# Head of a decoder trunk: half of c spread by a broadcast load, other buffers for the first adaLN tiles, operand parts made straight from x

## The chip, the core and the metric

The kernel runs on one core of one Trainium2 chip. The metric is device time in microseconds (us). A core has five engines that run side by side, each with its own list of instructions: TensorE (PE, matmuls; its weight loads are shown apart as PEld), VectorE (DVE), ScalarE (ACT), GpSimd (POOL) and SyncE (SP). Loads and stores are issued from the lists of SP, ACT and POOL and are carried out by 16 DMA engines. On-chip memory has 128 partitions; matmuls add up in PSUM banks.

## The reference

One layer on 512 tokens of width 2048: a token mixer (stick-breaking attention, sparse attention with a token indexer, gates) and a gated convolutional MLP, each behind an RMS norm whose scale and shift come from a condition vector c (adaLN). What matters here is the start:

```python
c_act = jax.nn.silu(c)
mod = c_act @ w_ada[layer] + b_ada[layer]
sh1, sc1, gt1, sh2, sc2, gt2 = jnp.split(mod[:, None, :], N_MOD, axis=-1)
h = rmsnorm(x, g_mix[layer]) * (1 + sc1) + sh1
...
proj = h @ w_in            # the indexer's queries qi are among its columns
```

## The kernel before, in words

Python code lists the work, tile by tile; a planner of the framework then puts the instructions on the engines' lists. It plays the program through with costs of its own and takes, of what is ready, what stands first in the code, so an engine's list need not have the order of the code. A buffer is asked for by a tag, and each tag has a fixed number of buffers: `raw` 8 (128 x 1024 numbers, 512 KB, for weights as loaded), `wh` and `wl` 3 each (a weight block's high and low part), `F` 62 (128 x 512), `ta`, `w`, `T` 2 each. An instruction that writes into a buffer waits until the last user of that buffer is done.

Matmuls are done in fp32 by parts. A number is written as a high part (rounded by ACT to the matmul type) and a low part (the rest, subtracted on DVE), and `mm3` does three matmuls: high by high, high by low, low by high. `parts` (L133, L135) makes both for a weight block, `split` (L162, L164) for an operand.

The head has these steps.

1. `c_spread` brings SiLU(c), 2048 numbers, into all 128 partitions, as two tiles `cb` of 1024 columns in `raw` buffers. c is loaded as two rows of one partition (L316). A matmul with a column of ones copies each 512 columns to all partitions (L322), ACT does the SiLU out of PSUM (L323). In the profile each of these four matmuls has two records. `cb` is kept, since later stages use it too.
2. An adaLN tile `t` gives 128 entries of `mod`: `ada_half` loads half of the tile's weights (128 x 1024, 512 KB) and multiplies it on DVE by `cb[half]` with a sum along the row (L290); `ada_end` adds the two sums and the bias (L304).
3. Loop over k = 0..15, the 128-row blocks of the model width. Tile 16 + k gives the scale of block k; `amp` (L385) is g_mix times one plus that scale. x of block k (256 KB) is loaded by `next_x`, one block ahead, and squared by ACT (L363), and the squares are added on DVE (L365). The operand of block k is x times amp in high and low part. Then a block of w_qi (128 x 896, 448 KB) is loaded and put into parts, and 21 matmuls of 512 columns add into seven PSUM banks. The norm's factor is applied later.
4. The next stage (`w_va`, 16 blocks) does the same with the normed x and eight banks, and makes the tiles of the shift beside it.

All loads named here are issued from the list of SP.

Of the kernel before, what the change touches and what calls it, by code (L numbers as in the profile page):

```python
# [10 lines left out]
F32 = mybir.dt.float32  # L11
F32R = mybir.dt.float32r
BF16 = mybir.dt.bfloat16
I32 = mybir.dt.int32
AF = mybir.ActivationFunctionType
ALU = mybir.AluOpType
PSUM = bass.MemoryType.PSUM

P = 128
D = 2048  # L20
S = 512
# [55 lines left out]
def block_kernel(ctx: ExitStack, tc: tile.TileContext, A: dict, out: bass.AP):  # L77
    nc = tc.nc
# [6 lines left out]
    def nm(s):  # L85
        counter[0] += 1
        return f"{s}_{counter[0]}"

    def t2k(tag, bufs, dt=F32, w=S):
        return sb.tile([P, w], dt, tag=tag, bufs=bufs, name=nm(tag))  # L90

    def slot(dt=F32):

        return t2k("F", SLOTS, dt)

    def acc():
        return pp.tile([P, S], F32, tag="acc", bufs=3, name=nm("acc"))
# [7 lines left out]
    mm = nc.tensor.matmul  # L105
    act = nc.scalar.activation
    tt = nc.vector.tensor_tensor
    ts = nc.vector.tensor_scalar
    stt = nc.vector.scalar_tensor_tensor
# [28 lines left out]
    def prep(src, w=1024):  # L138
        return parts(load(src, w), w)

    def mm3(ps, lhs, rhs, first, last, check=True):
        (ah, al), (bh, bl) = lhs, rhs
        mm(ps, ah, bh, start=first, stop=False, skip_group_check=not check)  # L143
        mm(ps, ah, bl, start=False, stop=False, skip_group_check=not check)  # L144
        return mm(ps, al, bh, start=False, stop=last, skip_group_check=not check)  # L145

    def cols(w, k, n=P):
        return tuple(x[:, k * n : (k + 1) * n] for x in w)
# [11 lines left out]
    def split(src, hi=None, lo=None):  # L160
        hi = slot(F32R) if hi is None else hi
        pins["hi"] = act(hi, src, AF.Copy)  # L162
        lo = slot(F32R) if lo is None else lo
        tt(lo, src, hi.bitcast(F32), ALU.subtract)  # L164
        return hi, lo
# [119 lines left out]
    amp = sb.tile([P, 2, KT], F32, tag="amp", name="amp")  # L285

    def ada_half(cb, t, half, tag=("raw", 8)):
        raw = t2k(*tag, w=1024)
        nc.sync.dma_start(raw, A["w_ada"][t * P : (t + 1) * P, half * 1024 : (half + 1) * 1024])
        return stt(raw, raw, 1.0, cb[half], ALU.mult, ALU.mult, accum_out=macc[:, t, half : half + 1])  # L290

    @contextmanager
    def behind(*pins):

        with ExitStack() as stack:
            for p in pins:
                stack.enter_context(tc.issue_after(p.ins))
            yield

    def ada_end(a, b):  # L300

        o = mod[:, a:b]
        if b - a == 1:
            stt(o, macc[:, a, 0:1], macc[:, a, 1:2], b_ada[:, a:b], ALU.add, ALU.add)  # L304
        else:
            tt(o, macc[:, a:b, 0], macc[:, a:b, 1], ALU.add)
            tt(o, o, b_ada[:, a:b], ALU.add)

    def c_spread():

        one = t2k("T", 2)[:1, :P]
        nc.vector.memset(one, 1.0)
        cb = []
        rows = [t2k("raw", 8, w=1024) for _ in range(2)]
        for half, row in enumerate(rows):
            nc.sync.dma_start(row[:1], A["c"][:, half * 1024 : (half + 1) * 1024])  # L316
        for row in rows:
            c = t2k("raw", 8, w=1024)
            for i in range(2):
                at = slice(i * S, (i + 1) * S)  # L320
                ps = acc()
                mm(ps, one, row[:1, at], start=True, stop=True)  # L322
                act(c[:, at], ps, AF.Silu)  # L323
            cb.append(c)
        return cb

    cb = c_spread()
    c_col = sb.tile([P, KT], F32, tag="c_col", name="c_col")
    nc.scalar.dma_start(c_col, A["c_col"])
# [3 lines left out]
    def rms(squares, blocks=range(NQB), bank=outs):  # L333

        total = bank()
        at = slice(blocks[0] * P, (blocks[-1] + 1) * P)
        for b in blocks:
            for i, t in enumerate(squares):
                mm(total[:, b : b + 1], t[:, b * P : (b + 1) * P], ones[:, :1], start=b == blocks[0] and i == 0,
                   stop=i == len(squares) - 1, skip_group_check=True)  # L340
        r = sb.tile([P, NQB], F32, tag="r", bufs=2, name=nm("r"))
        rb = r[:, blocks[0] : blocks[-1] + 1]
        act(rb, total[:, blocks[0] : blocks[-1] + 1], AF.Sqrt, scale=1.0 / D, bias=eps)
        nc.vector.reciprocal(rb, rb)
        wide = t2k("T", 2)
        for b in blocks:
            ts(wide[:, b * P : (b + 1) * P], ident, r[:, b : b + 1], None, ALU.mult)
        yield
        out = bank()
        mm(out[:, at], ones, wide[:, at], start=True, stop=True)  # L350
        yield out


    xt, total = [], None
# [3 lines left out]
    def next_x():  # L358
        x = slot()
        nc.sync.dma_start(x, A["x"][len(xt)])  # L360
        xt.append(x)
        sq = t2k("w", 2) if total else t2k("T", 2)
        act(sq, x, AF.Square)  # L363
        if total:
            tt(total, total, sq, ALU.add)  # L365
        return total or sq

    total = next_x()
    for k in range(KT):
        x = xt[k]  # L370
        if k == 6:
            past = t2k("w", 2)[:, :P]
            with behind(pins["load"]):
                nc.sync.dma_start(const, A["consts"][:, :5])
                nc.sync.dma_start(past, A["consts"][:, 5])
            nc.gpsimd.tensor_copy(mask[:, 0, :], ident)
            nc.gpsimd.tensor_copy(mask[:, 1, :], past)
        t = KT + k
        for half in range(2):
            ada_half(cb, t, half)  # L380
        if k == KT - 1:
            norm = rms([total])
            next(norm)
        ada_end(t, t + 1)
        stt(amp[:, 0, k : k + 1], mod[:, t : t + 1], 1.0, g_mix[:, k : k + 1], ALU.add, ALU.mult)  # L385
        h0 = t2k("ta", 2)
        act(h0, x, AF.Copy, scale=amp[:, 0, k : k + 1])
        h0 = split(h0)
        w = prep(A["w_qi"][k], NQ * P)
        for j in range(NQ):  # L390
            mm3(qi_ps[j], cols(w, j), h0, k == 0, k == KT - 1)
            if k == KT - 1 and j == 0:
                rstd = t2k("T", 2)
                act(rstd, next(norm), AF.Copy)
        for _ in range(2 if k == 8 else 1):
            if len(xt) < KT:
                total = next_x()
# [7 lines left out]
    def modulate(x, k, which, h, at=slice(0, S)):  # L405
        xn = t2k("w", 2)
        tt(xn[:, at], x[:, at], rstd[:, at], ALU.mult)
        act(h[:, at], xn[:, at], AF.Identity, scale=amp[:, which, k : k + 1],
            bias=mod[:, 48 * which + k : 48 * which + k + 1])
        return h  # L410
# [22 lines left out]
    for k in range(KT):  # L433
# [6 lines left out]
        w = prep(A["w_va"][k])  # L440
# [17 lines left out]
    ps = acc()  # L458
    for c in range(2):
        w = prep(A["w_tail"][c], 8 * TN)  # L460
# [7 lines left out]
    for j, (src, dst) in enumerate(((A["w_qi7"], qid[7]), (A["w_x0"][0], xd[0]), (A["w_x0"][1], xd[1]))):  # L468
        ps = (acc, att)[j % 2]()
        for c in range(2):  # L470
            w = prep(src[c])
            for k in range(8):
                i = 8 * c + k
# [494 lines left out]
    for j in range(KT):  # L968
        t = t2k("w", 2)
# [3 lines left out]
        ps = acc()  # L973
        w = prep(A["w_b"][j])
# [162 lines left out]
    for j in range(KT):  # L1137
# [5 lines left out]
        x = slot()  # L1143
# [15 lines left out]
    for p in range(KT // 2):  # L1159
        for k in (2 * p, 2 * p + 1):  # L1160
            if k < AHEAD:
                plain(k, [(L, modulated(k, L))], first_w[k])
            elif k % 2:
                x = split(modulate(x1[k], k, 1, x1[k]))
# [42 lines left out]
    for j in range(NU, NJ):  # L1207
        if j < 2 * NU:
            finish(j - NU, *ups[2 * (j - NU) : 2 * (j - NU) + 2])
        elif j < 2 * NU + 2:  # L1210
            x = t2k("T", 2)
# [10 lines left out]
    def bank(b):  # L1222
        return [att() for _ in range(4)] if b % 2 == 0 else [acc() for _ in range(3)] + [outs()]
# [202 lines left out]
    def rows_of(src):  # L1426

        both = [t2k("raw", 8, w=1024) for _ in range(2)]
        for v, r in enumerate(both):
            nc.sync.dma_start(r, src[:, v * 1024 : (v + 1) * 1024].to_broadcast([P, 1024]))  # L1430
        return [both[b // 2][:, b % 2 * S : (b % 2 + 1) * S] for b in range(4)]

    row, g_row = rows_of(gate_row), rows_of(A["g_row"])
# [19 lines left out]
    ps, before = [], None  # L1453
    x1_part = operands(0)
    for t in range(NQB):
# [3 lines left out]
        for b in range(4):  # L1459
            if not ps:  # L1460
                ps = bank(t)
# [3 lines left out]
            x = base[t, b]  # L1465
# [122 lines left out]
```

## Time and profile before

| what | value |
|---|---|
| median of 3 runs | 2807.38 us |
| lowest and highest run | 2806.15 and 2810.97 us |
| span of the profiled execution | 2805.4 us |
| mean granted TensorE clock | 0.997 |
| busy PE / DVE / ACT / POOL | 98% / 86% / 52% / 11% |
| DMA | 549.56 MB, mean 196 GB/s |

The span runs from the first to the last instruction of one execution; the profile gives no other time for that execution, and the median of the runs lies 2.0 us above it. A row of a timeline has the start, the duration, the engine, the line of code, the operation, `output<-inputs`, shapes and a count; in square brackets stand the idle time of the engine before it and what ended it. A row of groups has the busy time and the mean duration in ns at its end. In a row of DMA issues the last number is the time from issue to landing in us. `SPq` is the list of SP.

### The profile page before, as it was taken

What the parts mean: (1) busy time and instruction counts of PE and PEld (TensorE: products, weight loads), DVE (VectorE), ACT (ScalarE), POOL (GpSimd) and SP (SyncE); (2) the same over time, 40 slices, a digit from 0 to 9 for tenths busy, and PEclk for the clock granted to TensorE, in tenths of its full rate; (3) what the DMA queues carried; (4) which work ended last, traced back from release to release, by engine and by line L of the source; (5) the groups of instructions that cost most, each with busy time, mean ns of one, the idle gap of its engine ahead of it and who ended that gap; (6) DMA issues with size and microseconds to landing.
All of it is one profiled execution on the core that took longest, in us unless ns stands there. A gap on an engine that the chain in (4) does not pass through costs nothing.

```text
span 2805.4 us, 47711 instructions
## 1 busy us (share of the span) xinstructions
PE 2760.3 (98%) x18708; PEld 2533.1 (90%) x18708; DVE 2416.1 (86%) x3452; ACT 1464.4 (52%) x2062; POOL 314.4 (11%) x519
## 2 busy tenths in 40 slices
PE   9999999999999999999999999999999999999997
PEld 6779999999998768889999999999999998887875
DVE  8978978888887899788888998989898897888876
ACT  5544354455556655434466555555555455546452
POOL 0110000000002111112220000000000000002112
PEclk9999999999999999999999999999999999999998
DMA  9964456655556449766763666565666336468786
GB/s 358 363 231 135 150 173 211 203 180 166 184 198 220 145 168 314 246 215 191 235 222 116 184 168 175 166 175 167 173 166 173 118 121 213 156 181 240 200 241 195
DMA packets 164045, 549.56 MB, mean 196 GB/s; under 512 B 21398, under 2 KB 21782, under 8 KB 163820
## 3 DMA queue, kind: packets, MB, share of 16 engines
q1 hardware_dynamic: 116076, 404.82, 44.0%
q0 software_dynamic: 47152, 141.30, 17.9%
q8 instruction: 147, 2.41, 0.3%
q14 instruction: 78, 0.64, 0.1%
q10 hardware_dynamic: 592, 0.39, 0.0%
HBM read 453.19 MB, written 89.83 MB: 194 GB/s over the span
## 4 chain that ended last, share of the span: by engine, by line
PE 81%; DVE 10%; DMA 4%; issue 3%; ACT 1%; POOL 0%; DVEq 0%; ACTq 0%; POOLq 0%; SPq 0%
PE att L145 13%; PE att L143 12%; PE att L144 12%; PE acc L145 12%; PE acc L144 12%; PE acc L143 12%; DVE wl L135 2%; DVE raw L290 2%; DMA raw<-in_w_down 1%; DVE F L164 1%; PE acc L722 1%; PE acc L816 1%; PE outs L922 1%; DMA F<-sumd 1%; PE outs L144 1%
## 5 line engine op out<-in xcount | busy, mean ns | idle before, releaser
L133 ACT ACTIVATE wh<-raw 128x1024 fp32r<-128x1024 f32 (+2 forms) x792 | 832.4, 1052 | 1029.1 <-PE acc L144 192.8
L135 DVE TENSOR_TENSOR wl<-raw,wh 128x1024 fp32r<-128x1024 f32 (+2 forms) x792 | 956.2, 1210 | 142.2 <-ACT wh L133 133.6
L143 PE MATMUL acc<-F,wh 128*128 128x256 f32 (+1 forms) x2464 | 718.7, 294 | 6.4 <-ACT F L162 5.0
L145 PE MATMUL acc<-F,wl 128*128 128x256 f32 (+1 forms) x2464 | 721.7, 293 | 2.8 <-DVE wl L135 2.8
L144 PE MATMUL acc<-F,wh 128*128 128x256 f32 (+1 forms) x2464 | 721.9, 293 | 0.0
L145 PE MATMUL att<-F,wl 128*128 128x256 f32 (+1 forms) x2448 | 715.9, 292 | 2.4 <-DVE wl L135 2.4
L144 PE MATMUL att<-F,wh 128*128 128x256 f32 (+1 forms) x2448 | 715.8, 292 | 1.2 <-DVE F L164 1.2
L143 PE MATMUL att<-F,wh 128*128 128x256 f32 (+1 forms) x2448 | 711.8, 293 | 1.5 <-DVE sp L273 0.9
L143 PEld LDWEIGHTS acc<-F,wh 128*128 128x128 f32 x2464 | 471.4, 191 | 21.2 <-ACT F L162 6.8
L145 PEld LDWEIGHTS acc<-F,wl 128*128 128x128 f32 x2464 | 471.4, 191 | 13.3 <-DVE wl L135 3.8
L144 PEld LDWEIGHTS acc<-F,wh 128*128 128x128 f32 x2464 | 471.7, 191 | 11.5 <-DVE F L164 1.4
L143 PEld LDWEIGHTS att<-F,wh 128*128 128x128 f32 x2448 | 469.1, 192 | 12.9 <-issue 3.2
L144 PEld LDWEIGHTS att<-F,wh 128*128 128x128 f32 x2448 | 469.2, 192 | 12.2 <-DVE F L164 4.3
L145 PEld LDWEIGHTS att<-F,wl 128*128 128x128 f32 x2448 | 468.9, 192 | 11.4 <-DVE wl L135 3.4
L290 DVE SCALAR_TENSOR_TENSOR raw<-raw,raw 128x1024 f32<-128x1024 f32 x156 | 187.8, 1217 | 9.1 <-ACT raw L323 7.9
L143 PE MATMUL att<-wh,F 128*128 128x512 f32 x448 | 178.2, 398 | 1.1 <-ACT wh L133 1.1
L144 PE MATMUL att<-wl,F 128*128 128x512 f32 x448 | 175.0, 391 | 0.8 <-DVE wl L135 0.8
L145 PE MATMUL att<-wh,F 128*128 128x512 f32 x448 | 174.8, 390 | 0.0
L233 DVE TENSOR_TENSOR raw<-raw,raw 128x1024 f32<-128x1024 f32 x80 | 97.4, 1217 | 32.4 <-DMA raw<-in_w_o 17.5
L144 PE MATMUL acc<-wl,F 128*128 128x512 f32 x288 | 113.0, 392 | 2.5 <-DVE wl L135 2.5
L143 PE MATMUL acc<-wh,F 128*128 128x512 f32 x288 | 112.2, 391 | 0.5 <-ACT wh L133 0.5
L145 PE MATMUL acc<-wh,F 128*128 128x512 f32 x288 | 112.1, 389 | 0.0
(358 smaller groups left out, 3628.6 us busy)
## 6 DMA issues: line engine op xcount, KB each, us to landing
raw<-in_w_up SPq DMA_DIRECT2D x164, 512.0 KB, 3.6
raw<-in_w_ada SPq DMA_DIRECT2D x156, 512.0 KB, 5.2
raw<-in_w_x SPq DMA_DIRECT2D x128, 512.0 KB, 4.1
raw<-in_w_down SPq DMA_DIRECT2D x104, 512.0 KB, 4.6
xd<-F POOLq DMA_DIRECT2D x64, 256.0 KB, 2.5
F<-xd POOLq DMA_DIRECT2D x64, 256.0 KB, 5.2
raw<-in_w_o SPq DMA_DIRECT2D x32, 512.0 KB, 5.2
soft<-in_w_gate SPq DMA_DIRECT2D x32, 512.0 KB, 3.8
```

What stands on the lines that cost most here:

```text
L133: pins["wh"] = act(wh, raw, AF.Copy)
L135: pins["wl"] = tt(wl, raw, wh.bitcast(F32), ALU.subtract)
L143: mm(ps, ah, bh, start=first, stop=False, skip_group_check=not check)
L144: mm(ps, ah, bl, start=False, stop=False, skip_group_check=not check)
L145: return mm(ps, al, bh, start=False, stop=last, skip_group_check=not check)
L164: tt(lo, src, hi.bitcast(F32), ALU.subtract)
L233: last_v = tt(s, a21, a22, ALU.add)
L290: return stt(raw, raw, 1.0, cb[half], ALU.mult, ALU.mult, accum_out=macc[:, t, half : half + 1])
L722: mm(dots[:, :W], both[:, b * P : (b + 1) * P], kiR[i][:, :W], start=i == 0, stop=i == 1)
L816: mm(o, negtri if tri else negones, i, start=False, stop=True, skip_group_check=True)
L922: mm(o[:, b * P : (b + 1) * P], vs[kb][:, hd % 4 * HD : (hd % 4 + 1) * HD], pT[b][:, kb * P : (kb + 1) * P], start=kb == 0, stop=kb == b)
```

## The change

- Of c, only the first 1024 numbers are still loaded as rows (two of 512, in `F` buffers) and spread by matmuls. The second tile of `cb` is filled by a load that reads the same 4 KB row of memory for all 128 partitions (512 KB written), issued after the rows, and ACT then does the SiLU in place, 1024 columns at once.
- The halves of the first adaLN tile of the loop (k = 0) go into two `wl` buffers, those of the second (k = 1) into two `wh` buffers, in place of `raw`.
- The load of the first x is listed behind the first adaLN tile, no longer ahead of it.
- The operand's high part is written directly by ACT as x times amp in the matmul type; its low part is x times amp minus the high part, in one DVE instruction (`stt`, scalar_tensor_tensor, with amp as its column of scalars). Before, ACT wrote the product to a `ta` buffer, ACT copied it to the high part, and DVE subtracted (`tt`, tensor_tensor).

```diff
-        rows = [t2k("raw", 8, w=1024) for _ in range(2)]
-        for half, row in enumerate(rows):
-            nc.sync.dma_start(row[:1], A["c"][:, half * 1024 : (half + 1) * 1024])
-        for row in rows:
-            c = t2k("raw", 8, w=1024)
-            for i in range(2):
-                at = slice(i * S, (i + 1) * S)
-                ps = acc()
-                mm(ps, one, row[:1, at], start=True, stop=True)
-                act(c[:, at], ps, AF.Silu)
-            cb.append(c)
+        rows = [slot() for _ in range(2)]
+        for i, row in enumerate(rows):
+            nc.sync.dma_start(row[:1], A["c"][:, i * S : (i + 1) * S])
+        cb.extend(t2k("raw", 8, w=1024) for _ in range(2))
+        nc.sync.dma_start(cb[1], A["c"][:, 1024:].to_broadcast([P, 1024]))
+        for i, row in enumerate(rows):
+            ps = acc()
+            mm(ps, one, row[:1], start=True, stop=True)
+            act(cb[0][:, i * S : (i + 1) * S], ps, AF.Silu)
+        act(cb[1], cb[1], AF.Silu)
         return cb
...
-    total = next_x()
     for k in range(KT):
-        x = xt[k]
...
         for half in range(2):
-            ada_half(cb, t, half)
+            ada_half(cb, t, half, {0: ("wl", 3), 1: ("wh", 3)}.get(k, ("raw", 8)))
+        if not k:
+            total = next_x()
+        x = xt[k]
...
-        h0 = t2k("ta", 2)
-        act(h0, x, AF.Copy, scale=amp[:, 0, k : k + 1])
-        h0 = split(h0)
+        h0 = slot(F32R), slot(F32R)
+        act(h0[0], x, AF.Copy, scale=amp[:, 0, k : k + 1])
+        stt(h0[1], x, amp[:, 0, k : k + 1], h0[0].bitcast(F32), ALU.mult, ALU.subtract)
```

## The prediction

> **What bounds the kernel now.** I read the page first: TensorE (PE) is busy nearly always, so only a stretch in which it waits can give time.
>
> ```profile
> span 2805.4 us, 47711 instructions
> PE 2760.3 (98%) x18708; PEld 2533.1 (90%) x18708; DVE 2416.1 (86%) x3452; ACT 1464.4 (52%) x2062; POOL 314.4 (11%) x519
> ```
>
> Of the 45 us without PE, the view by stages shows where: six lie in the first 13.26 us, while the next long stage of the head is full on PE and almost full on VectorE (DVE). Columns: stretch, length, then busy time of PE, PEld, DVE, ACT and POOL, clock, DMA share, GB/s.
>
> ```profile
> 0.00:13.26 13.26, 7.16 (x8) 2.48 (x8) 4.52 (x10) 6.71 (x10) 0.20 (x4) 1.00 0.78 273
> 20.00:58.31 38.31, 38.31 (x170) 31.72 (x169) 37.93 (x73) 23.70 (x34) 1.68 (x2) 1.00 1.03 391
> ```
>
> Three resources are near their limits there: PE, DVE and the DMA engines (share 1.03 at 391 GB/s). Which one sets the end? The chain that ended last goes from the row load of c through the eight matmul records that spread it, then along DVE; later comes one long DMA wait.
>
> ```profile
> 0.74 1.41 DMA raw<-in_c
> 2.29 7.17 PE acc L322 x8
> 9.48 0.61 ACT raw L323
> ...
> 11.71 1.09 DVE wl L135
> ```
> ```profile
> 100.83 9.58 DMA raw<-in_w_va
> ```
>
> Between 11.71 and 100.83 us nearly every piece of it is DVE. So a microsecond that DVE starts earlier or works longer in the head shows at 100.83 us. That last load is issued when DVE frees a buffer, so its 9.58 us move with DVE. PE itself keeps a step of 4.76 us per k, seven times from 24.99 to 58.31, and stumbles where DVE has fallen behind: the next step is 5.07. So a slower DVE stream lengthens PE's steps too.
>
> ```profile
> 24.99 0.84 PE L143 MATMUL acc<-F,wh 128*128 128x512 f32 x3
> ...
> 58.31 0.84 PE L143 MATMUL acc<-F,wh 128*128 128x512 f32 x3
> 63.38 0.84 PE L143 MATMUL acc<-F,wh 128*128 128x512 f32 x3
> ```
>
> Then DVE's own start, in order of time: two products of the first adaLN tile with a hole of 2.18 us between them, mod, amp, the low part of the first w_qi, and the next tile.
>
> ```profile
> 6.70 1.22 DVE L290 SCALAR_TENSOR_TENSOR raw<-raw,raw 128x1024 f32<-128x1024 f32 x1 [5.67 <-ACT raw L323]
> 10.11 1.22 DVE L290 SCALAR_TENSOR_TENSOR raw<-raw,raw 128x1024 f32<-128x1024 f32 x1 [2.18 <-ACT raw L323]
> ...
> 11.71 1.09 DVE L135 TENSOR_TENSOR wl<-raw,wh 128x896 fp32r<-128x896 f32 x1
> 12.72 1.22 DVE L290 SCALAR_TENSOR_TENSOR raw<-raw,raw 128x1024 f32<-128x1024 f32 x1
> ```
>
> **The change, part by part.** *Spreading c.* Four of the eight matmul records go, but the first product needs the first four and their SiLUs as before, and it started at 6.70 right behind a SiLU: zero there. The second half comes by a 512 KB load and one SiLU of 1024 columns in place. Its price: two SiLUs of 512 columns take 2 x 0.61 (the chain's row at 9.48), the copy of a 896-wide block takes 0.95 (the row at 10.18 below); I take 1.1, near both. ScalarE (ACT) then waits for that load with the first w_qi's high part and the first operand queued behind it.
>
> When does the load land? The nearest rows are 256 KB of x, the first large load of the program, 2.8 us after its issue, and the two loads at the end that spread g_row in the same shape, 6.9 us.
>
> ```profile
> F<-in_x SPq DMA_DIRECT2D x1, 256.0 KB, 2.8
> ```
> ```profile
> raw<-in_g_row SPq DMA_DIRECT2D x2, 512.0 KB, 6.9
> ```
>
> Issued third, at about 1.5 us, it lands between 4.3 and 8.4 us, with its SiLU done by 9.5 at the latest. The Trainium skill's page "DMA: Bandwidth & Descriptors" (section "Anatomy of one DMA — SWDGE (gpsimd) path") fits 2.0 us plus the bytes at 436 GB/s, an estimate of 3.2 us here, for another issuing engine; it would land at 4.7 us and leave the sum below as it is.
>
> *The DMA queue.* The view of issues and their landings says what the second product could really have had. The second half of the first tile was issued at about 2.3 us and needed 6.7, the next tile's first half was issued at 3.25 and needed 8.2. Columns of the first fence: start, duration.
>
> ```profile
> 1.43 0.35 SPq L360 DMA_DIRECT2D F<-in_x  x1
> 1.83 0.90 SPq L289 DMA_DIRECT2D raw<-in_w_ada  x2
> ...
> 3.25 3.14 SPq L289 DMA_DIRECT2D raw<-in_w_ada  x2
> ```
> ```profile
> raw<-in_w_ada SPq DMA_DIRECT2D x2, 512.0 KB, 6.7
> ```
> ```profile
> raw<-in_w_ada SPq DMA_DIRECT2D x1, 512.0 KB, 8.2
> ```
>
> So it landed at about 9.0, and the hole before 10.11 is DMA for half of its length, whatever the row of waits names. After the change this half has the 512 KB of c ahead of it and no longer the 256 KB of x. At the rates of these stretches
>
> ```profile
> 3.00:4.00 1.00, 1.00 (x2) 0.33 (x1) 0.00 (x0) 0.21 (x1) 0.00 (x0) 1.00 1.03 342
> ...
> 8.00:9.00 1.00, 1.00 (x2) 0.00 (x0) 0.00 (x0) 0.37 (x1) 0.00 (x0) 1.00 1.01 407
> ...
> 10.00:11.00 1.00, 0.00 (x0) 0.00 (x0) 0.89 (x1) 0.90 (x2) 0.00 (x0) 1.00 0.85 214
> 11.00:12.00 1.00, 0.00 (x0) 0.00 (x0) 0.93 (x5) 0.30 (x2) 0.00 (x0) 1.00 0.76 262
> ```
>
> 512 KB (0.524 MB) is 1.3 to 1.5 us and 256 KB half of it. The second product can start at 9.0 + 0.7 = 9.7, 0.4 us earlier than now. But w_qi's first block, which had x and the tile ahead of it, now has the 512 KB more ahead: it lands 1.4 us later. It followed the half tile in its queue, so it landed between 9.0 and the 10.18 at which its copy began; 9.0 plus its 0.459 MB at 0.4 MB/us is 10.1.
>
> ```profile
> 10.18 0.95 ACT L133 ACTIVATE wh<-raw 128x896 fp32r<-128x896 f32 x1
> 11.83 0.72 ACT L387 ACTIVATE ta<-F,amp 128x512 f32<-128x512 f32 x1 [0.70 <-DVE amp L385]
> 12.58 0.63 ACT L162 ACTIVATE F<-ta 128x512 fp32r<-128x512 f32 x1
> ```
>
> 10.1 + 1.4 + 0.95 = 12.45 for wl in place of 11.71: DVE stands from 11.3 to 12.45, since the next tile (3.25 + 8.2 = 11.45 now) also lands 1.4 later, at 12.85. **First term: DVE's steady stream starts 0.7 us later.** Bounds: 2.19 us earlier (the whole hole from 7.92 to 10.11 gone and nothing else late) and 1.4 later (a full 512 KB). I take the value that the landings give.
>
> *The weight parts' buffers.* The first two tiles free four raw buffers, so later loads can go out sooner: DMA ran at 214 and 262 GB/s from 10 to 12 us because the SP queue stood for buffers. Against 0.4 MB/us that is 0.32 MB not moved, less than the 0.52 MB added. It keeps the delay from growing; I count no gain. Each first part of a w_qi block still finds one of three wl and wh buffers free; the second block's wh needs one of the second tile's, free after its product. If it had to wait for the first block's matmuls instead, it would cost about one step of PE, 5 us.
>
> *The x load behind the first tile.* It lands at 1.43 + 2.8 = 4.2 now; its first hard use is the operand at 11.83. Three loads of 512 KB come ahead of it, about 4 to 5 us more, and it is needed only once mod and amp have followed the second product of 9.7 to 10.9: at 11.3. Zero.
>
> *The operand parts.* Per k, one ACTIVATE of 0.63 us goes, 16 in all; ACT is busy 23.70 of 38.31 us and hides that. On DVE the TENSOR_TENSOR of the low part becomes a SCALAR_TENSOR_TENSOR whose scalar is a column, amp. The rows by line tell these apart:
>
> ```profile
> L164 DVE TENSOR_TENSOR F<-ta,F 128x512 fp32r<-128x512 f32 x16 | 11.0, 690 | 0.0
> ```
> ```profile
> L798 DVE SCALAR_TENSOR_TENSOR soft<-acc,soft 128x512 f32<-128x512 f32 x16 | 10.9, 682 | 9.1 <-ACT soft L791 9.1
> L1009 DVE SCALAR_TENSOR_TENSOR F<-F,mod,w 128x512 f32<-128x512 f32 x14 | 10.5, 748 | 0.2
> ```
>
> With a constant it takes 682 ns, with a column 748. **Second term: 16 x 0.06 = +0.9 us**, all on the engine that carries the chain. The Trainium skill's page "VectorE: DVE Perf Modes" (section "The TRN2 errata — SBUF-src ops pay a fixed extra latency per instruction") gives one formula, (N+151)/0.96 ns, for an fp32 tensor_tensor and no term for a scalar. By that, 691 ns, the term would be zero and the sum 0.9 less (2808.1, inside the forecast's own range); the L164 row agrees with the formula, the row with a column lies 57 ns above it, and the row decides.
>
> **Sum.** +0.7 + 0.9 = +1.6 us on a span of 2805.4. The profile gives a span only; the median of the runs, 2807.38 (2806.15 to 2810.97), stands 2.0 above it, and I add the sum to the median: 2809.0 us. Differences under 0.2% (5.6 us) are about what a measurement here cannot tell from no change. The sum is far inside that.
>
> **Rivals.** *The hole closes.* The landing of 9.0 may come from a laggard engine and not recur; then the second product starts at 7.92, -2.19 + 0.9 = -1.3, or 2806.1. For it: the waits name the SiLU, and x took 2.8 us. Against: the order in the queue. Even so DVE idles only 2.3 us between 6.70 and 13.26 (6.56 less some 4.3 of the 4.52 busy), so the head alone cannot give 0.2%.
>
> *The second tile's loads go last (slower).* The program's order isn't the queue's: x of the next k, which the code names ahead of the second tile, is issued at 10.33, among the third tile's loads.
>
> ```profile
> 10.33 0.42 SPq L360 DMA_DIRECT2D F<-in_x  x1
> ```
>
> If the planner gives out wh in the order of the code, the second tile's loads wait for the first wh and fall behind five raw loads (two w_qi, three half tiles; 2.49 MB, 6.4 us at 391 GB/s). DVE would then get that tile at 12.85 + 6.4 = 19.25 instead of 12.72: +6.5 + 0.9 = 7.4, or 2814.8. It decides if DVE's order has nothing to put ahead; from 1.8 MB on it passes 0.2%. Against: the third tile's products would then be there to fill DVE.
>
> *The planner's order shifts later on.* Costs and due times move at the head, and with them perhaps a wait far behind it. The longest in the chain is
>
> ```profile
> 1426.84 10.43 DMA F<-x1d
> ```
>
> one such wait more or less is 2818 or 2797. Nothing in the change touches it.
>
> **How the numbers follow.** Forecast 0.56, hole closes 0.24 (both within 0.2%), second tile last 0.09 (slower), order elsewhere 0.11 (0.07 faster, since waits are there to lose, 0.04 slower). So faster 0.07, same 0.80, slower 0.13. The forecast's own range is 2807 to 2811. The range for all runs from the hole closed, taken from the fastest run (2806.15 - 1.3 = 2804.9), to the forecast's upper bound (1.4 + 0.9) on the slowest run, 2813.3: 2804.5 to 2813.5.
>
> **What would show it.** The low part of h0 at about 0.75 us in place of 0.69; the second product at 9 to 10 us; wl of the first block near 12.4; the spreading load landed before 8.4; PE's steps still 4.76 with longer stumbles; the w_va load that waits now issued 1 to 2 us after 100.8. I am wrong if the second product starts near 8, if DVE's stream is interrupted after 13 us, or if the stages behind 113 us change by more than the head.

## The result, and the profile after

The changed kernel takes 2761.53 us (median of 5 runs, 2757.82 to 2768.14) against 2807.01 (2805.48 to 2810.97): ratio 0.9841, 95% interval 0.983 to 0.9851. It is 1.6% faster, where no change was forecast, and outside the range of 2804.5 to 2813.5.

The two head lines of the page after:

```profile
span 2757.5 us, 47708 instructions
PE 2697.6 (98%) x18704; PEld 2457.7 (89%) x18704; DVE 2411.3 (87%) x3452; ACT 1450.7 (53%) x2045; POOL 315.3 (11%) x519
```

PE does the same matmuls (four fewer records) in 62.7 us less busy time, at a mean granted clock of 0.995 (0.997 before). Its waits grew: span less busy was 45.1 us and is 59.9. So the gain is in how long matmuls take, and some of it has come back as waits.

Where along the span? Three landmarks that both kernels have are the norms' small DVE instructions; the last numbers of a row are the starts of the first and last of them. Before:

```profile
L347 DVE TENSOR_SCALAR T<-const,r x4: 280/280/286, 85.8 to 86.4; 128x128 f32<-128x128 f32 x4
L1034 DVE TENSOR_SCALAR T<-const,r x4: 280/280/286, 1434.2 to 1442.5; 128x128 f32<-128x128 f32 x4
L1442 DVE TENSOR_TENSOR r<-s x4: 160/161/163, 2764.1 to 2797.4; 128x2 f32<-128x2 f32 x4
```

After:

```profile
L346 DVE TENSOR_SCALAR T<-const,r x4: 279/280/282, 94.6 to 95.2; 128x128 f32<-128x128 f32 x4
L1034 DVE TENSOR_SCALAR T<-const,r x4: 281/281/286, 1430.4 to 1438.5; 128x128 f32<-128x128 f32 x4
L1442 DVE TENSOR_TENSOR r<-s x4: 160/161/163, 2716.2 to 2749.6; 128x2 f32<-128x2 f32 x4
```

Up to the first norm the changed kernel is 8.8 us *later*. Up to the second it has made that good and is 3.8 ahead, and between the second and the last it gains 44.1 more. The head, which the change is about, lost 8.8 us; the code behind it, which the change does not touch, gained 56.7.

A window of 100 us in the longest of those stretches, in which PE never waits, before and then after (columns as in the prediction's table by stages):

```profile
1700.00:1800.00 100.00, 100.00 (x836) 100.00 (x835) 88.91 (x105) 55.48 (x70) 6.84 (x10) 1.00 0.63 172
```
```profile
1700.00:1800.00 100.00, 100.00 (x885) 100.00 (x884) 93.99 (x112) 58.46 (x75) 7.08 (x10) 1.00 0.67 178
```

836 matmuls became 885: 119.6 ns each became 113.0, with the clock at 1.00 in both. The timeline of PE shows it row by row, before:

```profile
1700.00 0.28 PE L145 MATMUL att<-F,wl 128*128 128x256 f32 x1
1700.12 0.28 PE L143 MATMUL att<-F,wh 128*128 128x256 f32 x1
1700.24 0.28 PE L144 MATMUL att<-F,wh 128*128 128x256 f32 x1
```

and after:

```profile
1699.98 0.28 PE L145 MATMUL acc<-F,wl 128*128 128x256 f32 x1
1700.09 0.28 PE L143 MATMUL acc<-F,wh 128*128 128x256 f32 x1
1700.21 0.28 PE L144 MATMUL acc<-F,wh 128*128 128x256 f32 x1
```

The duration in the row (0.28) is the same and says nothing, since matmuls overlap; the step from start to start is what counts. Over the whole trace the 13,700 such steps of 256 columns (F as the moving tile, wh or wl as weights; stalls left out) have a mean of 120.0 ns before and 114.1 after: 80 us less. Matmuls of 512 columns got longer: 1,340 with F moving went from 227.5 to 233.2 ns and 2,410 with F as weights from 227.2 to 229.2, 12 us together. 80 - 12 is 68, close to the 62.7 us that the page shows for PE's busy time.

What could make the same instruction faster? The change asks for an `F` buffer (the rows of c) before the first `raw` buffer, and the tags get their places in SBUF in the order in which they are first asked for. So the tiles moved. Byte addresses within a partition, from the two built programs:

```
          T      F (62 x 2048)   raw      c_col    wh       wl       wh - F, wl - F mod 256
before    22816  59744           26912    59680    190816   203104   0, 0
after     22816  26912           153888   186656   199008   186720   64, 64
```

The 64 bytes of c_col used to lie below F and now lie between F and the weight parts. That gives **theory A**: the step depends on the distance in SBUF between a matmul's moving tile and its weights. The rivals were **B**, F's own place, and **C**, the planner's changed order of the work behind the new head.

### The profile page after: what moved, and what is told of

Its sections match the earlier page's. It is cut to its first block, busy times and chain, and to the rows that moved or that the text cites. A ratio compares the mean times of both kernels' runs of the same rounds, so it can differ in the third digit from the quotient of the medians.

```text
span 2757.5 us, 47708 instructions
## 1 busy us (share of the span) xinstructions
PE 2697.6 (98%) x18704; PEld 2457.7 (89%) x18704; DVE 2411.3 (87%) x3452; ACT 1450.7 (53%) x2045; POOL 315.3 (11%) x519
## 4 chain that ended last, share of the span: by engine, by line
PE 67%; DVE 8%; DMA 5%; issue 4%; ACT 1%; POOL 0%; DVEq 0%; POOLq 0%; ACTq 0%; SPq 0%
PE att L145 10%; PE att L143 10%; PE att L144 10%; PE acc L145 10%; PE acc L143 10%; PE acc L144 10%; DVE wl L135 3%; DMA raw<-in_w_x 1%; DMA raw<-in_w_down 1%; PE acc L722 1%; PE acc L816 1%; PE outs L922 1%; DMA raw<-in_w_o 1%; PE outs L145 1%; PE outs L144 1%
## 5 line engine op out<-in xcount | busy, mean ns | idle before, releaser
L143 PE MATMUL acc<-F,wh 128*128 128x256 f32 (+1 forms) x2464 | 709.1, 290 | 12.8 <-ACT wh L133 7.1
L145 PE MATMUL acc<-F,wl 128*128 128x256 f32 (+1 forms) x2464 | 710.6, 289 | 6.1 <-DVE wl L135 6.1
L144 PE MATMUL acc<-F,wh 128*128 128x256 f32 (+1 forms) x2464 | 710.3, 288 | 0.6 <-DVE F L388 0.4
L143 PE MATMUL att<-F,wh 128*128 128x256 f32 (+1 forms) x2448 | 704.8, 289 | 5.8 <-DVE sp L273 4.5
L145 PE MATMUL att<-F,wl 128*128 128x256 f32 (+1 forms) x2448 | 704.2, 288 | 3.3 <-DVE wl L135 3.0
L144 PE MATMUL att<-F,wh 128*128 128x256 f32 (+1 forms) x2448 | 704.5, 288 | 1.2 <-DVE F L164 1.2
L143 PEld LDWEIGHTS acc<-F,wh 128*128 128x128 f32 x2464 | 463.3, 188 | 29.5 <-ACT wh L133 12.2
L145 PEld LDWEIGHTS acc<-F,wl 128*128 128x128 f32 x2464 | 463.0, 188 | 19.2 <-DVE wl L135 8.5
L143 PEld LDWEIGHTS att<-F,wh 128*128 128x128 f32 x2448 | 460.4, 188 | 19.3 <-ACT wh L133 5.2
L144 PEld LDWEIGHTS acc<-F,wh 128*128 128x128 f32 x2464 | 463.8, 188 | 12.9 <-DVE F L388 1.4
L144 PEld LDWEIGHTS att<-F,wh 128*128 128x128 f32 x2448 | 461.3, 188 | 13.6 <-DVE F L164 4.3
L145 PEld LDWEIGHTS att<-F,wl 128*128 128x128 f32 x2448 | 460.3, 188 | 14.3 <-DVE wl L135 5.0
L290 DVE SCALAR_TENSOR_TENSOR raw<-raw,raw 128x1024 f32<-128x1024 f32 x152 | 182.1, 1217 | 0.0
```

## The experiments

**Distance alone, in both directions (b_pad64, a_rel0).** The first is the kernel before with 64 unused bytes above F:

```diff
     total = next_x()
+    pad = sb.tile([P, 16], F32, tag="pad", name="pad")
+    nc.gpsimd.memset(pad, 0.0)
```

> The kernel before, its head untouched, with one unused tile of 64 bytes a partition put between the tag F and the tags ta, wl and wh, so that a wl or wh buffer stands 64 bytes (mod 512) off an F buffer instead of 0. Theory A (a float32r matmul's rate depends on the distance in SBUF between its weights and its moving tile): the 256-column steps go from 120 to 113 ns, the 512-column ones from 227 to 229-233 ns, and the time falls by 13,800 x 6.5 ns less 4,100 x 4 ns, about 70 us at most and 50 as far as other engines let it: 2740 to 2760 us, no slower than the changed kernel, because the old head stays. Theory B (F's own address, 59744 before and 26912 after, sets the rate): F has not moved, 120 ns and 2807 us. Theory C (the planner's order of the work behind the new head): the order is that of before, 2807 us.

2757.06 us, ratio 0.9823 [0.9807, 0.9839]. The same window:

```profile
1700.00:1800.00 100.00, 100.00 (x885) 100.00 (x884) 93.99 (x111) 56.82 (x73) 7.63 (x11) 1.00 0.67 183
```

The second is the changed kernel with c_col created first:

```diff
-    cb = c_spread()
     c_col = sb.tile([P, KT], F32, tag="c_col", name="c_col")
+    cb = c_spread()
```

> The changed kernel with the 64-byte tile c_col created ahead of the spreading of c, so that it lies below F and no longer between F and wl, wh: F moves by 64 bytes, wl and wh keep their addresses, and the distance is 0 mod 512 again. Nothing that an engine executes differs. Theory A: steps of 120 and 227 ns again, and the time of before plus what the new head costs (its matmuls ran some 9 us late at 300 us): 2808 to 2818 us. Theory B, if it is F's region of SBUF: 113 ns and 2761 us; if it is F's place mod 128 (96 before, 32 after, 96 here): 120 ns too, which b_pad64 tells from A. Theory C: 2761 us.

2809.74 us, ratio 1.0017 [1.0007, 1.0026].

```profile
1700.00:1800.00 100.00, 100.00 (x836) 100.00 (x835) 89.03 (x105) 54.96 (x71) 7.07 (x10) 1.00 0.62 168
```

An unused tile gives the old kernel the whole gain; taking the accident out of the changed kernel takes the whole gain away and leaves the head's loss. B and C fall: in the first F stands where it stood, in the second PE's order is that of the changed kernel. The weight parts' own place falls too: in the second they stand where they stand in the changed kernel, and only F has moved, by 64 bytes.

**Which distances (b_pad32, b_pad96, b_off128, b_off256, b_off192, b_al64).** b_pad32 and b_pad96 have 8 and 24 columns in the pad. The next two create amp (128 bytes) or macc (768) behind the first F; b_off192 is b_off128 with the 64-byte pad added; b_al64 is b_pad64 with 32 unused bytes below F. The edit of b_off128:

```diff
-    amp = sb.tile([P, 2, KT], F32, tag="amp", name="amp")
...
     total = next_x()
+    amp = sb.tile([P, 2, KT], F32, tag="amp", name="amp")
```

> The kernel before with an unused tile of 32 bytes between F and wl, wh: distance 32 mod 512. Theory A with a bank of 64 bytes or more: as before, 120 ns and 2807 us; with one of 32 bytes: 113 ns and 2740 to 2760 us; a step in between would mean that the cost falls off gradually with the distance. Theories B and C: 2807 us.

> The kernel before with an unused tile of 96 bytes between F and wl, wh: distance 96 mod 512. Theory A: at 64 bytes the conflict may be gone in part only (10 to 20% of the steps still took 117-118 ns); if it falls off with the distance, 96 gives under 113 ns and a time below that of the 64-byte tile, by up to 20 us; if it is all or nothing, the same as 64. Theories B and C: 2807 us.

> The kernel before with the 128-byte tile amp created behind the first F tile instead of ahead of it: F moves down by 128 bytes, wl and wh stay, distance 128 mod 512; nothing that an engine executes differs. So far a distance of 0 gave 120.0 ns a 256-column step, 32 gave 118.3, 64 gave 114.8, 96 gave 118.4 (means without stalls). Theory A1 (any multiple of 64 but 0 keeps the two streams apart): about 114-115 ns and 2755 to 2760 us. Theory A2 (the pattern repeats every 128 bytes): 120 ns and 2806 us. Theory A3 (64 is only half the way, the rest of the 117-118 ns steps goes with more distance): 113 ns throughout, 512-column steps at 227, 2740 to 2750 us.

> The kernel before with the 768-byte tile macc created behind the first F tile: F moves down by 768 bytes, wl and wh stay, distance 256 mod 512. A1 and A3: as with 128, or between 64 and 128. If the pattern repeats every 256 bytes: 120 ns and 2806 us, whatever 128 gives.

> The kernel before with the 128-byte tile amp and an unused one of 64 bytes created behind the first F tile: distance 192 mod 256, that is minus 64. Measured so far, mean 256-column step without stalls: distance 0 120.0 ns, 32 118.3, 64 114.8, 96 118.4, 128 118.7, 256 120.0: a period of 256. If the rate depends on the distance alone and is even in it, 192 does what 64 does: 114-115 ns and 2757 us, with the 512-column steps exchanged (229 ns where F is the moving tile, 233 where it is the stationary one, since wl and wh against F at 64 gave 229 the other way round). If what counts is which of the two streams is ahead: 118-120 ns and 2806 us.

> The kernel before with an unused tile of 32 bytes below F and one of 64 between F and wl, wh: distance 64 as in b_pad64, but F, wl and wh all start at a multiple of 64 bytes, where all runs so far had F at 32 mod 64. Distance alone: 114.8 ns, 2757 us as b_pad64. If the 117-118 ns steps (some 30% in b_pad64, 15% in the changed kernel) come from tiles that straddle 64-byte lines: 113 ns throughout and 10 to 20 us less, 2737 to 2747 us.

All that was measured on distance, with the three kernels of the next paragraph. The fourth column is the mean step of 256 columns, the fifth those of 512 columns (F moving, F as weights), counted from the traces with stalls left out; each ratio is against the kernel before on the same chip in the same session (medians 2806.0 to 2808.4 us):

| kernel | wh - F, wl - F mod 256 | matmuls from 1700 to 1800 us | 256 columns, ns | 512 columns, ns | median us | ratio, 95% interval |
|---|---|---|---|---|---|---|
| before | 0, 0 | 836 | 120.0 | 227.5, 227.2 | 2807.0 | |
| a_rel0 | 0, 0 | 836 | 120.0 | 227.6, 227.2 | 2809.7 | 1.0017 [1.0007, 1.0026] |
| b_off256 | 0, 0 (256 mod 512) | 835 | 120.0 | 227.5, 227.2 | 2806.0 | 0.9999 [0.999, 1.0007] |
| b_pad32 | 32, 32 | 847 | 118.3 | 233.2, 233.3 | 2804.2 | 0.9995 [0.9985, 1.0004] |
| after | 64, 64 | 885 | 114.1 | 233.2, 229.2 | 2761.5 | 0.9841 [0.983, 0.9851] |
| b_pad64 | 64, 64 | 885 | 114.8 | 233.2, 229.2 | 2757.1 | 0.9823 [0.9807, 0.9839] |
| b_al64 | 64, 64 | 885 | 114.8 | 233.3, 229.3 | 2757.6 | 0.9817 [0.9801, 0.9833] |
| b_pad96 | 96, 96 | 845 | 118.4 | 234.0, 233.4 | 2803.3 | 0.9988 [0.9979, 0.9998] |
| b_off128 | 128, 128 | 845 | 118.7 | 232.9, 232.7 | 2806.7 | 1.0001 [0.9993, 1.001] |
| b_off192 | 192, 192 | 851 | 117.6 | 229.2, 233.3 | 2791.4 | 0.9943 [0.9931, 0.9956] |
| b_wl64 | 0, 64 | 852 | 117.8 | 230.8, 232.0 | 2793.6 | 0.9956 [0.9943, 0.9969] |
| b_wh64 | 64, 0 | 852 | 118.4 | 231.9, 233.0 | 2802.5 | 0.9983 [0.9973, 0.9992] |
| b_wh64_wl128 | 64, 128 | 848 | 118.2 | 231.1, 231.9 | 2798.8 | 0.9973 [0.9962, 0.9984] |

The pattern repeats after 256 bytes, as far as one pair of distances can tell, and not after 128: the steps of b_off256 are those of before, the steps of b_off128 are not. The guess that the cost falls off with the distance was wrong (96 is worse than 64), and so were all three of the theories written for 128: its step is neither 120 nor 113 but 118.7. Its longer steps of 512 columns eat up what it gains, so that the 2806 us of theory A2 came out by luck. Minus 64 (192) exchanges the two kinds of 512-column steps, as expected, but leaves the 256-column ones at a mean of 117.6. Where the tiles stand mod 64 does not matter (b_al64). Only 64 for both parts gives 113 ns for long: at 192 some 4% of the steps, in short stretches, take 113.4 ns, and 95% take 117.8 (means of 12 steps in a row).

**One weight part alone (b_wl64, b_wh64, b_wh64_wl128).** In the order F, wh, wl the 64 bytes go between wh and wl; in b_wh64 wl is asked for first; in b_wh64_wl128 c_col is created behind the first F as well. The edit of b_wl64:

```diff
         wh = t2k("wh", 3, F32R, w)
+        if "wh" not in pins:
+            pad = sb.tile([P, 16], F32, tag="pad", name="pad")
+            nc.gpsimd.memset(pad, 0.0)
         pins["wh"] = act(wh, raw, AF.Copy)
         wl = t2k("wl", 3, F32R, w)
```

> The kernel before with the unused tile of 64 bytes between wh and wl: wh stays at distance 0 of F, wl stands at 64. The 256-column matmuls come in threes: wh with F's high part (L146 here), wh with its low part (L147), wl with the high part (L148). If the step is slowed by loading the next matmul's weights while the running one reads its moving tile, the steps that lead to an L148 (its wl is loaded during L147) take 113-118 ns and the two others 120. If it is the matmul's own weights, L148's own steps are the short ones. If it needs both, all three stay at 120 or all three go. One step of three shorter by 2 to 7 ns is 4,575 steps, 9 to 32 us less a few us of longer 512-column steps: 2775 to 2800 us.

> The kernel before with wl's buffers first (distance 0 of F) and, behind 64 unused bytes, wh's (distance 64): the mirror of b_wl64, in which all steps took 117.8 ns. Two of three matmuls have wh as weights. If the distance of wh, or of the majority, decides: 113-118 ns in spells, as with both at 64, 2755 to 2780 us. If any weights at distance 0 hold the whole train back: 117.8 ns and 2793 us as b_wl64.

> The kernel before with c_col created behind the first F tile (wh at distance 64) and 64 unused bytes between wh and wl (wl at 128); both at 128 gave 118.7 ns, both at 64 113.3 or 117.8 in spells. If the worse of the two decides: 118-119 ns and about 2800 us. If what counts is that the streams differ from one another: 113.3 ns throughout and 2735 to 2750 us.

b_wl64 took 2793.59 us:

```profile
1700.00:1800.00 100.00, 100.00 (x852) 100.00 (x851) 90.08 (x107) 55.73 (x71) 7.08 (x10) 1.00 0.64 174
```

Of its three expectations the last came nearest, that all three steps go together: the steps of a triple have means of 117.5, 117.5 and 118.3 ns, whichever weights come next or are in use. In b_wh64 83% of the steps go at the same 117.8 ns, as its second alternative said. But 15% of them, most between 625 and 850 us, take 122.2, longer than at distance 0, and the time is 2802.5 us and not 2793:

```profile
700.00:800.00 100.00, 100.00 (x820) 100.00 (x819) 86.61 (x103) 57.42 (x79) 10.05 (x19) 1.00 0.57 176
```

b_wh64_wl128 came out as its first alternative said, that the worse of the two decides (118.2 ns, 2798.8 us), though there the steps of a triple are less alike (119.0, 119.5 and 116.2). So one part at distance 0 or 128 holds the whole train of matmuls at about 118 or above, even where the other stands at 64. Which two accesses get in each other's way, no run here shows.

**Two paces at distance 64 (b_pad64_again, after_again).** The same programs once more, side by side on another chip.

> The kernel b_pad64 once more, beside the changed kernel on one chip: 2757 us by the first time, with a spread of 10 us as the share of 117-118 ns steps varies.

> The changed kernel once more beside b_pad64_again, distance 64 in both. By the offsets of the matmuls in the traces (3.4 us at the head's start, 4.7 at the norm behind it, 4.4 left at 1600 us) it is 4 us slower than b_pad64; by the prediction's two terms 1.6 us.

2760.78 us (2754.98 to 2782.21, ratio 0.9843 [0.9819, 0.9868]) and 2776.41 (2771.32 to 2780.57, ratio 0.9895 [0.9882, 0.9908]). The changed kernel is 15 us slower than in its first session, with not one instruction different, and 15.6 us behind b_pad64, where 4 or 1.6 were expected; b_pad64 spread by 27 us and not by 10. The trace of the changed kernel shows why:

```profile
1700.00:1800.00 100.00, 100.00 (x851) 100.00 (x850) 90.63 (x107) 56.50 (x72) 7.08 (x10) 1.00 0.65 176
```

In the first session this window held 885 matmuls, here 851. Followed in pieces of 25 us, the step at distance 64 is either 113.3 or 117.8 ns and keeps that for tens to hundreds of microseconds; the long train from about 1600 to 2120 us ran at 113.3 in the first trace of the changed kernel and at 117.8 in this one. Some 4,500 steps times 4.5 ns are 20 us, and the spans differ by 16.9. The same train ran at 113.3 in both traces of b_pad64. What sets the pace when a train begins stays open. So b_pad64 and b_al64, which has the same head, are the fastest versions found. Where b_pad64 and the changed kernel ran together it leads by 2761 to 2776 us, but a good part of that lead is the pace of this one train and not the head.

**The head's parts (h_head, h_stt, h_t2raw).** All have distance 64. h_head is the changed kernel with the old operand parts; h_stt is b_pad64 with the new ones; h_t2raw keeps the second adaLN tile in `raw`:

```diff
-            ada_half(cb, t, half, {0: ("wl", 3), 1: ("wh", 3)}.get(k, ("raw", 8)))
+            ada_half(cb, t, half, {0: ("wl", 3)}.get(k, ("raw", 8)))
```

> The changed kernel with the low part of h0 taken as before (the scaled x into a tile of ta, then the split with its plain subtraction), everything else of the change kept; distance 64 as in the changed kernel. By the prediction's second term it gains 0.9 us on the changed kernel: 2760.6; against b_pad64 (old head, distance 64, 2757.1) it then stands 3.5 us back, which would be the head's loads, where the first term said 0.7. Rival: the low part costs nothing, since DVE is not what sets the end in this stage: 2761.5.

> The kernel b_pad64 (old head, distance 64) with the changed low part alone (hi and lo into F tiles, lo by SCALAR_TENSOR_TENSOR from x). Second term: 2757.1 + 0.9 = 2758.0 us, the two-product rhythm of DVE longer by 0.06 us a step; rival: no difference within 1 us in the sum of the 16 steps, since the steps wait for loads and not for DVE. Its tag ta now comes behind wl and wh in SBUF; distance is 64 still, so steps of 114-115 ns either way.

> The changed kernel with its second adaLN tile in the raw buffers instead of wh; the first stays in wl. In the changed kernel the matmuls run 3.4 us behind those of b_pad64 (same distance, old head) from the second step on, and the second tile's loads were issued at 5.90 us behind loads of later tiles. By the rival of the prediction (second tile's loads go last) the second tile's products come sooner by 3 us and the first offset goes from +3.4 to about 0: total 2758 us. If the broadcast load of c is what costs it: still +3.4 and 2761.

Medians 2764.33 us (2758.26 to 2787.13), 2762.38 (2755.27 to 2791.23) and 2778.82 (2760.93 to 2792.09): the two paces move these totals by more than the parts of the head are worth, so the totals tell nothing here. The traces do. Start of the same-numbered matmul against b_pad64 (mm3's matmuls counted from 0), in us:

| kernel | 50th | 250th | 350th | 900th |
|---|---|---|---|---|
| after | +3.4 | +3.4 | +8.1 | +6.9 |
| h_t2raw | -0.9 | +2.0 | +6.3 | +6.7 |
| h_stt | +0.5 | +1.3 | +6.7 | +6.1 |
| h_head | +5.1 | +5.1 | +9.8 | +8.6 |

There are two losses. The first comes before the 50th and is the second tile in `wh`: without it the head is 0.9 us *ahead* of the old one there, though 2.0 us behind it by the 250th. The second, about 5 us, comes near the 300th, where the norm's factor is made. ACT's copy of that factor in b_pad64 and in h_stt:

```profile
90.63 0.60 ACT L396 ACTIVATE T<-outs 128x512 f32<-128x512 f32 x1 [1.84 <-PE outs L350]
```
```profile
96.43 0.60 ACT L396 ACTIVATE T<-outs 128x512 f32<-128x512 f32 x1 [4.96 <-PE outs L350]
```

In the changed kernel it is at 98.48, and PE's eight small matmuls that begin the norm, at 84.26 us before, stand at 92.10:

```profile
92.10 0.95 PE L338 MATMUL outs<-const,T 128*128 128x1 f32 x8
```

The planner had put them later on PE's list: 301 matmuls of mm3 stand ahead of them before and in b_pad64, 315 in the others, two thirds of a block more. Each of the two halves of the change alone brings that about (h_stt and h_head both have it); what in the planner's costs does it was not tried. Both losses are there without any difference in distance: a_rel0 against the kernel before is at +3.9, +3.7, +7.4 and +6.3 us at the same four matmuls.

## Why the prediction was wrong

**The step that failed** is an unspoken one, that a matmul costs after the change what it cost before, so that the stages behind the head stay as they are. In its place the runs showed 114.1 ns for 120.0 in 13,700 steps, by the distance alone. The prediction counted queues, landings and instructions, and no address. Its own last sentence named the sign of it, "if the stages behind 113 us change by more than the head". The rival "the planner's order shifts later on", which had 0.07 on the faster side, has the place right (far behind the head) and the mechanism wrong: a_rel0 has the changed order and none of the gain. Nothing in the trace of before had shown the price, because all its steps of this kind stood at 120.0 ns; a distance that never varies leaves no second row to compare with. With the distance kept at 0 the total comes near the forecast: a_rel0 takes 2809.74 us, where the sum gave 2809.0. That is partly luck. a_rel0 stands 3.7 us above the kernel before beside it (2.0 to 7.3 by the interval), where the sum said +1.6, and neither of the two terms behind the sum came out.

**First term, +0.7 us.** The head after, in order of time:

```profile
5.70 1.06 ACT L323 ACTIVATE raw<-raw 128x1024 f32<-128x1024 f32 x1 [0.64 <-DMA raw<-in_c]
5.90 2.73 SPq L289 DMA_DIRECT2D wh<-in_w_ada  x2
8.40 1.23 DVE L290 SCALAR_TENSOR_TENSOR wl<-wl,raw 128x1024 f32<-128x1024 f32 x1 [7.38 <-DMA wl<-in_w_ada]
9.57 1.23 DVE L290 SCALAR_TENSOR_TENSOR wl<-wl,raw 128x1024 f32<-128x1024 f32 x1
12.04 0.75 DVE L388 SCALAR_TENSOR_TENSOR F<-F,amp,F 128x512 fp32r<-128x512 f32 x1 [0.79 <-ACT F L387]
12.88 1.09 DVE L135 TENSOR_TENSOR wl<-raw,wh 128x896 fp32r<-128x896 f32 x1
13.89 1.22 DVE L290 SCALAR_TENSOR_TENSOR raw<-raw,raw 128x1024 f32<-128x1024 f32 x1
15.74 1.23 DVE L290 SCALAR_TENSOR_TENSOR wh<-wh,raw 128x1024 f32<-128x1024 f32 x1
```

The spreading load landed by 5.70, inside its bounds of 4.3 to 8.4, and its SiLU took 1.06 (1.1 was said). The second product stands at 9.57 (9 to 10). The first was to stay at 6.70, and that was wrong: it waits for its own weights, behind the 512 KB of c, until 8.40. The hole between the two products closed mostly because the first came 1.70 us later; the second came 0.54 us sooner. The w_qi low part came at 12.88 (12.45 said), and the first matmul at 12.90 was even 0.36 us earlier than before. By the 50th matmul the head is far behind, though: 3.9 us in a_rel0, where the term said 0.7. Most of the difference is the next rival.

**The rival "second tile's loads go last"**, which had 0.09, happened in part. The loads into wh were issued at 5.90, behind raw ones, their product ran at 15.74 (19.25 by the rival, 12.72 before), and DVE did put the third tile ahead (13.89), as the argument against it said. h_t2raw prices it at 4.3 us at the 50th matmul and at 1.4 by the 250th, where the rival had +6.5.

**PE's step of 4.76 us** was to stay, and became 4.90, as the timeline of PE after shows:

```profile
38.20 0.86 PE L143 MATMUL acc<-F,wh 128*128 128x512 f32 x3
43.10 0.86 PE L143 MATMUL acc<-F,wh 128*128 128x512 f32 x3
```

Over 21 matmuls that is 233 ns each and no longer 227: the price of distance 64 for 512 columns, not DVE's. b_pad64, with the old head, has the same 4.90, and a_rel0, at distance 0, has 4.76.

**Second term, +0.9 us.** The low part takes 0.75 us, as read from the row with a column as scalar (748 ns). What failed is "all on the engine that carries the chain". In a_rel0, whose matmuls take as long as before, the offset against the kernel before is 3.9 us at the 50th matmul and 3.4 at the 300th: twelve blocks with the longer low part cost nothing there. In h_stt PE's step stays at the 4.90 us of b_pad64 too; between the 50th and the 250th matmul it falls back by 0.8 us, nearly all of it at one wait:

```profile
65.36 0.97 PE L143 MATMUL acc<-F,wh 128*128 128x512 f32 x3 [0.50 <-ACT F L389]
```

The shorter way to the operand (one ACT instruction fewer) is worth more than the low part costs. With the old operand parts in the new head (h_head), which by this term were to gain 0.9 us, the 50th matmul starts 1.7 us later still. The start of the second block shows it, in h_head and then in the changed kernel:

```profile
22.93 0.96 PE L143 MATMUL acc<-F,wh 128*128 128x512 f32 x3 [2.52 <-ACT F L162]
```
```profile
22.31 0.73 PE L143 MATMUL acc<-F,wh 128*128 128x512 f32 x2 [1.47 <-ACT F L387]
```

That gain was costed at nothing with the words that ACT hides it; while the head starts up, it does not.

**The wait in w_va.** The load behind the 9.58 us wait, the fourth of w_va, was to be issued 1 to 2 us after 100.83. It was issued 6.3 us after it, behind the norm, whose delay no part of the prediction foresaw:

```profile
107.14 0.33 SPq L126 DMA_DIRECT2D raw<-in_w_va  x1
```

The chain after can't be set against the one before here: followed back, it ends at 386 us and does not reach the head.

**Where the rest of the gain went.** PE's busy time fell by 62.7 us and the span by 47.9; the 14.8 us between them are new waits of PE. Two stretches hold nearly all of it, the first 225 us and the next 675, each before and then after:

```profile
0.00:225.00 225.00, 217.81 (x921) 172.24 (x922) 190.77 (x345) 122.26 (x181) 16.58 (x33) 1.00 0.83 300
225.00:900.00 675.00, 671.90 (x5402) 659.28 (x5401) 583.90 (x781) 337.58 (x450) 60.31 (x112) 1.00 0.56 185
```
```profile
0.00:225.00 225.00, 210.16 (x875) 164.73 (x876) 188.72 (x340) 103.23 (x143) 16.35 (x32) 0.99 0.83 300
225.00:900.00 675.00, 664.94 (x5467) 646.58 (x5466) 588.75 (x793) 350.26 (x479) 62.08 (x115) 1.00 0.59 188
```

In the first, where the head's two losses lie, 7.2 us of waits became 14.8. In the second 3.1 became 10.1, though a_rel0, with the new head at distance 0, waits only 1.4 there: a faster PE stands more often for what DVE makes (4.3 us for wl, 3.8 for the tiles sp, in the waits of that stretch after).

## What to carry to other kernels

A change of the order in which buffers are first asked for moves every tile behind them, and on this kernel 64 bytes of layout were worth some 49 us, more than ten times the 3.7 that the edit itself cost. So when a time moves in stages that a change doesn't touch, compare the step from start to start of equal instructions, then the addresses, and undo the shift alone before any story is told about the edit. And keep a pad as an experiment of its own: here the old head with 64 unused bytes is at least as fast as the whole change.

## What the runs showed of the hardware

The step of a float32r matmul of 256 columns depended on the distance in SBUF between the moving tile and its weights: 120.0 ns at 0 and at 256, 118.3 to 118.7 at 32, 96 and 128, a mean of 117.6 at 192, and 113.3 or 117.8 at 64. Matmuls of 512 columns went the other way: 227 ns at 0 and 229 to 234 elsewhere. At 64 the pace of a train is one of two values and stays for tens to over 500 us. Other layouts have a second pace too: 113.4 for 4% of the steps at 192, and 122.2 for 15% of them with wh at 64 and wl at 0. Runs of one program at distance 64 spread by up to 36 us (h_stt, 2755.27 to 2791.23), runs at distance 0 by 5 to 10; that the pace makes this spread is shown by one pair of traces (after, after_again) and not run by run. The granted clock was 1.00 in the windows from 1700 to 1800 us of all these kernels.
